# The order in which the residual's tiles are loaded for the down product of a SwiGLU sub-layer

## The chip, the cores and the metric

The kernel runs on one core of a Trainium2 chip. The metric is the device time of one execution in microseconds (us). Five engines work side by side: TensorE (PE in the profile, with its weight loads as PEld), VectorE (DVE), ScalarE (ACT), GpSimd (POOL) and SyncE (SP), which here issues almost every DMA. Each engine works its instructions off in the order in which they stand in the program.

## The reference, cut to what matters

The layer has a SwiGLU half-step at its start and another at its end. x has 1024 tokens of 1024 columns, the inner width is 2816, all in float32.

```python
def swiglu(h, w_gate, w_up, w_down):
    return (jax.nn.silu(h @ w_gate) * (h @ w_up)) @ w_down
...
        h = modulate(rms_norm(x, norm_ffn1[l]), mod[:, 0], mod[:, 1])
        x = x + 0.5 * mod[:, 2][:, None, :] * swiglu(h, ffn1_gate[l], ffn1_up[l], ffn1_down[l])
...
        h = modulate(rms_norm(x, norm_ffn2[l]), mod[:, 6], mod[:, 7])
        x = x + 0.5 * mod[:, 8][:, None, :] * swiglu(h, ffn2_gate[l], ffn2_up[l], ffn2_down[l])
```

The x that is added to is the residual. The product with w_down, and the sum with the residual, are the place of the change.

## The kernel before

Everything is held transposed: a tile has 128 columns of the layer (a row tile d, 0 to 7) and 512 tokens (a half h, 0 or 1). The residual is thus 16 tiles A[d, h] of 256 KB. While the gate and up products run, their place on the chip is needed for other things, so the residual waits in DRAM (`xpark` in the first half-step, `rest` in the second) and is loaded back for the down product.

The down product works on a pair p of row tiles (2p and 2p + 1) at a time and on both halves. It saves one block product in eight: `seven` makes seven products p1, p2, p5, p6, p3, p7 and q4 of sums and differences of blocks, each over a few pairs of inner tiles at once (an entry of the plan: the first four entries, for p = 0, 1, 2, 3, take 2, 3, 3 and 4 inner tiles). A float32 product is three matmuls of split values, so a product over 3 inner tiles is 9 matmuls. In the order of TensorE an entry's p1 stands ahead of the q4 of the entry before; then come the entry's p2, p5, p6, p3 and p7.

After a product, VectorE adds what stands in its PSUM bank, times fg (half the modulation vector), to a tile of the residual: `down_read`. p1 and p2 go to A[2p, 0], p5 to A[2p+1, 1], p6 and p3 to A[2p, 1], p7 to A[2p+1, 1] and q4 to A[2p+1, 0]. Products share banks: p6, p7 and q4 go on adding in the bank of p1 (`mm` in the profile), p3 in the bank of p5 (`po`). So p6 can't start before p1 has been read out, and p3 can't start before p5 has been read out; the read can't happen before its tile of the residual is there.

A tile of the residual takes one of 16 places called A0 to A15. Until shortly before, these hold values of the gate and up products, and some of them come free late: `direct_task` writes the last inner tiles straight from such a place (the VectorE instructions that write zs, G and H in the rows below) and gives it back. `feed_task` starts the loads, four tiles for each of the pairs 0 to 3, and feeds the ring of inner tiles (U, zs, G and H, loaded from `gd` in DRAM). `rest_load` waits for a free place, then issues its DMA.

The order of the work on each engine is made ahead of time: `Order` is a small planner that runs all tasks against estimated durations and writes down each engine's instructions in the order of its clock; tasks that wait for the same place get it in the order in which they were started. TensorE, VectorE and ScalarE keep that order. The order of the DMAs on SyncE's queue follows from when each can be issued.

Of the kernel before, what the change touches and what calls it, by code (L numbers as in the profile page):

```python
# [35 lines left out]
class Order:  # L36
# [18 lines left out]
    def spawn(self, gen, rank):  # L55
        self.seq += 1
        self.tasks.append({"gen": gen, "rank": rank, "seq": self.seq, "ready": self.t, "ask": None, "last": None, "end": self.t})
        return self.tasks[-1]
# [84 lines left out]
def hybrid_layer_kernel(  # L143
# [209 lines left out]
    spawn, put, mark = order.spawn, order.put, order.set  # L353

    def need(what, n=1):
        return ("need", what, n)

    def flag(*key):
        return ("flag", key)
# [22 lines left out]
    def temp(dt=F32):  # L382

        i = max(free, key=lambda i: (i % 8, i))
        free.remove(i)
        return i, atile(i, dt)
# [5 lines left out]
    def arrive(key, us=2.5):  # L392
        yield ("wait", us)
        mark(key)
# [357 lines left out]
    for st in range(2):  # L752
# [6 lines left out]
        for t in range(2 * NS):  # L759
            d = t % 4  # L760
# [358 lines left out]
    def place_of(v, r):  # L1119
        if v == "p5":  # L1120
            return utile(F32R), ztile(F32R)
        if v in ("p6", "p7"):
            return tuple(gtile((0 if v == "p6" else 8) + 2 * r + e, F32R) for e in range(2))
        ht = htile(r + (4 if v in ("p2", "p3") else 0), 1 if v in ("p3", "q4") else 0)
        return ht[:, 0], ht[:, 1]
# [17 lines left out]
    def feed_task(st):  # L1143

        for p in range(NPAIR):
            r = p % 4
            if p < 4:
                for d in (2 * p, 2 * p + 1):
                    for h in range(2):
                        spawn(rest_load(st, d, h), 2.5)  # L1150
            if p in DIRECT:
                continue
            for v in SLOTS if p < NS else ((0, 0), (0, 1), (1, 0), (1, 1)):
                place = v if p < NS else {(0, 0): "p1", (1, 0): "p2", (1, 1): "p3", (0, 1): "q4"}[v]
                if p < 4:
                    yield flag("vfree", st, place)
                else:
                    yield flag("gfree", st, p - 4, place)
                yield flag("gd", st, p, v)
                key = (st, p, v) if p < NS else (st, p, *v)  # L1160
                for e in range(2):
                    yield ("D", 0.78)
                    if e == 0:
                        ring[key] = place_of(place, r)
                    nc.sync.dma_start(out=ring[key][e].bitcast(F32), in_=gdram[st, p, v][:, e])
                spawn(arrive(("G", *key)), 3)

    def rest_load(st, d, h):

        yield flag("vfree", st, "p1")  # L1170
        while ("cut", st) not in order.flags and len(free) < 5:
            yield ("wait", 0.5)
        yield need("tmp")
        A[d, h] = temp()[1]
        yield ("D", 0.78)
        nc.sync.dma_start(out=A[d, h], in_=rest[st][d, h])
        spawn(arrive(("rest", st, (d, h))), 3)
# [861 lines left out]
    for st in range(2):  # L2039
        spawn(combine_task(st), 1.5)  # L2040
        for j in range(NPAIR):
            spawn(parts_task(st, j), 3.5)
        spawn(feed_task(st), 2.5)
# [41 lines left out]
```

## Time and profile before

| | |
|---|---|
| time, median of 3 runs | 1838.82 us (1838.65 to 1839.89) |
| time of the profiled execution | 1837.93 us |
| its span in the profile | 1836.2 us |
| mean granted TensorE clock | 0.996 of full |
| TensorE busy | 1791.9 us (98%) |
| VectorE busy | 1398.9 us (76%) |
| ScalarE busy | 759.8 us (41%) |
| GpSimd busy | 282.1 us (15%) |

Busy is the time in which an engine had an instruction in work. The profiled execution took 1.73 us more than its span, and 0.89 us less than the median. Times of single instructions are from the start of the span.

### The profile page before, as it was taken

Reading aid. Unit: us, or ns where it says so; the run is one execution under the profiler, and the core shown is the slowest. Engines: PE = TensorE matmul, PEld = TensorE weight load, DVE = VectorE, ACT = ScalarE, POOL = GpSimd, SP = SyncE. Lnnn points to the kernel's source line nnn. Section 1 sums busy time; section 2 is a strip of 40 time slices with the busy share of each in tenths; the row PEclk is TensorE's granted clock in tenths of the full one; section 3 lists DMA queues with packets and bytes.
Section 4 is the critical chain, followed back from the end, with each engine's and each line's share of the span. In section 5 each row is a group of like instructions: output and inputs, shape, how many; then the busy total and the mean of one; then the engine's idle time right before and its main releaser. Section 6 shows DMA issues by size and latency. Waiting matters only on the chain.

```text
span 1836.2 us, 25080 instructions
## 1 busy us (share of the span) xinstructions
PE 1791.9 (98%) x8527; PEld 1481.6 (81%) x8527; DVE 1398.9 (76%) x2434; ACT 759.8 (41%) x1504; POOL 282.1 (15%) x224
## 2 busy tenths in 40 slices
PE   7999999999999999999999999999999999999998
PEld 6788878888878876788888878888878888878877
DVE  5997888887769877988786666687787666776666
ACT  5454444443422224562443254354444444422223
POOL 2221121201100004120211122212211111100003
PEclk9999999999999999999999999999999999999999
DMA  9534676574679923321122155334455543758722
GB/s 326 176 127 161 217 223 196 184 231 134 204 227 337 320 87 118 104 74 48 27 52 50 35 164 156 100 125 155 150 189 169 185 152 110 228 179 274 235 76 98
DMA packets 307807, 293.81 MB, mean 160 GB/s; under 512 B 28061, under 2 KB 215506, under 8 KB 307680
## 3 DMA queue, kind: packets, MB, share of 16 engines
q1 hardware_dynamic: 307136, 291.09, 49.9%
q8 instruction: 67, 1.10, 0.3%
q0 software_dynamic: 544, 1.13, 0.2%
q14 instruction: 60, 0.49, 0.1%
HBM read 209.05 MB, written 83.10 MB: 159 GB/s over the span
## 4 chain that ended last, share of the span: by engine, by line
PE 85%; DVE 10%; issue 2%; ACT 1%; POOL 1%; DMA 1%; DVEq 0%; POOLq 0%; SPq 0%; ACTq 0%
PE mm L161 48%; PE po L161 27%; PE aux L161 7%; PE rec L161 3%; DVE pm L161 2%; DVE ad L161 2%; DVE A L161 1%; DVE split L161 1%; DVE G L161 1%; DVE cv L161 1%; DVE zs L161 0%; DVE H L161 0%; ACT A L161 0%; DMA G<-in_conv_w 0%; ACT junk L161 0%
## 5 line engine op out<-in xcount | busy, mean ns | idle before, releaser
L161 PE MATMUL mm<-H,split 128*128 128x512 f32 (+1 forms) x3096 | 759.2, 393 | 3.6 <-DVE A L161 3.6
L161 PEld LDWEIGHTS mm<-H,split 128*128 128x128 f32 x3096 | 566.4, 188 | 118.2 <-ACT split L161 4.6
L161 PE MATMUL po<-H,split 128*128 128x512 f32 x1584 | 390.2, 394 | 8.2 <-DVE A L161 6.1
L161 PEld LDWEIGHTS po<-H,split 128*128 128x128 f32 x1584 | 298.9, 190 | 73.4 <-ACT split L161 6.4
L161 PE MATMUL mm<-G,split 128*128 128x512 f32 x1440 | 342.3, 389 | 0.0
L161 PEld LDWEIGHTS mm<-G,split 128*128 128x128 f32 x1440 | 270.7, 188 | 56.3
L161 ACT CAST split<-pm 128x512 fp32r<-128x512 f32 (+3 forms) x264 | 151.7, 582 | 323.5 <-DVE pm L161 305.9
L161 POOL TENSOR_TENSOR A<-A,A 128x512 f32<-128x512 f32 x80 | 130.9, 1646 | 681.1 <-DVE A L161 456.9
L161 DVE TENSOR_TENSOR split<-pm,split 128x512 fp32r<-128x512 f32 (+3 forms) x264 | 176.7, 676 | 44.9 <-ACT split L161 44.5
L161 ACT CAST split<-raw 128x512 fp32r<-128x512 f32 (+3 forms) x199 | 117.6, 595 | 189.2 <-PE mm L161 106.4
L161 PE MATMUL po<-U,split 128*128 128x512 f32 x480 | 155.5, 390 | 2.1 <-DVE A L161 2.0
L161 DVE SCALAR_TENSOR_TENSOR A<-mm,fg,A 128x512 f32<-128x512 f32 (+1 forms) x144 | 103.4, 720 | 57.6 <-PE mm L161 55.8
L161 DVE TENSOR_TENSOR split<-raw,split 128x512 fp32r<-128x512 f32 (+3 forms) x199 | 131.6, 672 | 20.3 <-ACT split L161 19.9
L161 DVE TENSOR_TENSOR A<-A,A 128x512 fp32r<-128x512 f32 (+1 forms) x180 | 125.1, 703 | 4.0 <-ACT A L161 1.2
L161 PEld LDWEIGHTS po<-U,split 128*128 128x128 f32 x480 | 90.1, 188 | 22.0 <-issue 1.7
L161 ACT CAST split<-cv 128x512 fp32r<-128x512 f32 (+2 forms) x96 | 57.1, 595 | 91.5 <-PE po L161 55.8
L161 DVE TENSOR_TENSOR A<-A,po 128x512 f32<-128x512 f32 x86 | 58.8, 684 | 45.7 <-PE po L161 43.8
L161 PE MATMUL po<-zs,split 128*128 128x512 f32 x240 | 93.5, 390 | 0.0
L161 DVE SCALAR_TENSOR_TENSOR A<-po,fg,A 128x512 f32<-128x512 f32 x78 | 58.3, 749 | 37.6 <-PE po L161 37.3
L161 DVE SCALAR_TENSOR_TENSOR ad<-ad,cs,ad 128x512 f32<-128x512 f32 x98 | 82.8, 845 | 2.2 <-DMA ad<-in_w_ada 1.2
L161 DVE TENSOR_TENSOR split<-cv,split 128x512 fp32r<-128x512 f32 (+2 forms) x96 | 62.7, 653 | 28.3 <-ACT split L161 28.3
L161 ACT CAST A<-A 128x512 fp32r<-128x512 f32 x120 | 72.7, 619 | 25.3 <-DVE A L161 25.2
(270 smaller groups left out, 1856.4 us busy)
## 6 DMA issues: line engine op xcount, KB each, us to landing
gd<-A SPq DMA_DIRECT2D x240, 256.0 KB, 3.8
H<-gd SPq DMA_DIRECT2D x144, 256.0 KB, 4.3
ad<-in_w_ada SPq DMA_DIRECT2D x112, 256.0 KB, 3.1
raw<-in_ffn_gate SPq DMA_DIRECT2D x88, 256.0 KB, 3.9
cv<-in_ffn_up SPq DMA_DIRECT2D x80, 256.0 KB, 4.3
G<-gd SPq DMA_DIRECT2D x64, 256.0 KB, 4.7
raw<-in_w_in SPq DMA_DIRECT2D x40, 256.0 KB, 3.1
raw<-in_w_out SPq DMA_DIRECT2D x32, 256.0 KB, 3.1
```

What stands on the lines that cost most here:

```text
L161: ins = f(*args, **kwargs)
```

## The change

The four tiles of a pair are started in another order: before (2p, 0), (2p, 1), (2p+1, 0), (2p+1, 1), now (2p, 0), (2p+1, 1), (2p, 1), (2p+1, 0). This is the order in which the products p1, p5, p6 and q4 first read them. It holds for all four pairs and both half-steps.

```diff
             if p < 4:
-                for d in (2 * p, 2 * p + 1):
-                    for h in range(2):
-                        spawn(rest_load(st, d, h), 2.5)
+                for d, h in ((2 * p, 0), (2 * p + 1, 1), (2 * p, 1), (2 * p + 1, 0)):
+                    spawn(rest_load(st, d, h), 2.5)
```

The places come free at the same points as before, so what moves is which tile gets which place, and with it the planner's order. The order of TensorE's, ScalarE's and GpSimd's instructions is the same in both kernels; VectorE's differs in one stretch of some 20 instructions in each half-step. Both stretches are around the second entry with 3 inner tiles (p = 2, row tiles 4 and 5).

SyncE's queue in the first half-step, from the first load for row tiles 4 and 5 that stands late on. In DRAM, xpark_778 is A[4, 1], 723 is A[5, 0], 785 is A[5, 1]; 735, 792, 744 and 798 are A[6, 0], A[6, 1], A[7, 0] and A[7, 1]. A[4, 0] was loaded long before in both kernels. Before:

```order
L1176 DMA A_969_4726<-xpark_778 128x512
L1176 DMA A_972_4743<-xpark_723 128x512
...
L1176 DMA A_989_4830<-xpark_785 128x512
L1176 DMA A_990_4836<-xpark_735 128x512
L1176 DMA A_991_4841<-xpark_792 128x512
L1176 DMA A_994_4850<-xpark_744 128x512
L1176 DMA A_995_4861<-xpark_798 128x512
L1165 DMA H_0_1002_4904<-gd_1793 128x512 x2
```

The same place of the queue in the changed kernel:

```order
L1175 DMA A_969_4726<-xpark_785 128x512
L1175 DMA A_972_4743<-xpark_778 128x512
...
L1175 DMA A_989_4830<-xpark_723 128x512
L1175 DMA A_990_4844<-xpark_735 128x512
L1175 DMA A_993_4862<-xpark_798 128x512
L1164 DMA H_0_1000_4898<-gd_1793 128x512
L797 DMA cv_4892<-in_ffn_down 128x3x128
L1164 DMA H_0_1000_4898<-gd_1793 128x512
L1175 DMA A_1001_4904<-xpark_792 128x512
...
L1175 DMA A_1008_4937<-xpark_744 128x512
```

A[5, 1] has moved from the third to the first of these loads, A[4, 1] from the first to the second, A[5, 0] from the second to the third; the loads of A[6, 1] and A[7, 0] now stand among the loads of the ring and of weights.

VectorE's order at the same entry; po_4806 is the bank of p5 and p3, mm_4750 the bank of p1, p6 and p7, and the A in a row is the residual's tile that is added to. Before:

```order
L161 TENSOR_TENSOR zs_4629<-A_917_4525,U_4628 128x512
L161 TENSOR_TENSOR G_948_4638<-A_923_4544,G_947_4637 128x512
L161 TENSOR_TENSOR H_1_953_4654<-A_880_4331,H_1_953_4654 128x512
L161 TENSOR_TENSOR split_4825<-cv_4716,split_4825 128x512
L161 SCALAR_TENSOR_TENSOR A_969_4726<-mm_4750,fg_164,A_969_4726 128x512
L161 TENSOR_TENSOR pm_4844<-cv_4686,cv_4701 128x512
L161 TENSOR_TENSOR G_956_4667<-A_890_4377,G_955_4666 128x512
L161 SCALAR_TENSOR_TENSOR A_989_4830<-po_4806,fg_164,A_989_4830 128x512
```

In the changed kernel:

```order
L161 TENSOR_TENSOR zs_4629<-A_917_4525,U_4628 128x512
L161 SCALAR_TENSOR_TENSOR A_969_4726<-po_4806,fg_164,A_969_4726 128x512
L161 TENSOR_TENSOR split_4825<-cv_4716,split_4825 128x512
L161 TENSOR_TENSOR G_948_4638<-A_923_4544,G_947_4637 128x512
L161 SCALAR_TENSOR_TENSOR A_972_4743<-mm_4750,fg_164,A_972_4743 128x512
L161 TENSOR_TENSOR pm_4849<-cv_4686,cv_4701 128x512
L161 TENSOR_TENSOR H_1_953_4654<-A_880_4331,H_1_953_4654 128x512
L161 SCALAR_TENSOR_TENSOR A_972_4743<-po_4806,fg_164,A_972_4743 128x512
```

The read of p5 (the first with po_4806) has moved from behind the read of p6 (with mm_4750) to six instructions earlier, straight behind the instruction that writes zs; the read of p3 now stands where the read of p5 stood.

## Rows read from the trace of the kernel before

**Rows 1.** The page, part 1: busy us (share of the span) and instructions of TensorE.

```profile
PE 1791.9 (98%) x8527; PEld 1481.6 (81%) x8527; DVE 1398.9 (76%) x2434; ACT 759.8 (41%) x1504; POOL 282.1 (15%) x224
```

**Rows 2.** Waits of TensorE, whole span: us in total, times, longest us.

```profile
PE po L161 <- DVE A L161: 8.2, 6, 2.8
```

**Rows 3.** Timeline of TensorE, first half-step: start, us, what [idle before].

```profile
507.32 2.20 PE L161 MATMUL po<-H,split 128*128 128x512 f32 x9
...
511.40 2.20 PE L161 MATMUL mm<-G,split 128*128 128x512 f32 x9
516.40 3.67 PE L161 MATMUL po<-H,split 128*128 128x512 f32 x9 [2.80 <-DVE A L161]
519.87 2.49 PE L161 MATMUL mm<-G,split 128*128 128x512 f32 x9
522.20 4.93 PE L161 MATMUL mm<-H,split 128*128 128x512 f32 x21
...
545.33 2.20 PE L161 MATMUL po<-H,split 128*128 128x512 f32 x9
```

**Rows 4.** The chain that ended last, 455 to 560: start, us, what.

```profile
509.56 0.63 DVE A L161
...
510.23 0.55 DVE split L161
510.78 0.61 DVE zs L161
...
511.41 2.82 DMA A<-xpark
...
514.31 0.68 DVE pm L161
514.99 0.60 DVE G L161
515.59 0.67 DVE A L161
```

**Rows 5.** Timeline of VectorE, same place.

```profile
513.64 0.75 DVE L161 SCALAR_TENSOR_TENSOR A<-mm,fg,A 128x512 f32<-128x512 f32 x1 [0.46 <-PE mm L161]
...
520.11 0.75 DVE L161 SCALAR_TENSOR_TENSOR A<-po,fg,A 128x512 f32<-128x512 f32 x1 [2.66 <-PE po L161]
```

**Rows 6.** Timeline of SyncE's DMA issues, same place.

```profile
499.23 2.35 SPq L1176 DMA_DIRECT2D A<-xpark  x2
...
511.41 6.39 SPq L1176 DMA_DIRECT2D A<-xpark  x5
523.08 0.79 SPq L1165 DMA_DIRECT2D H<-gd  x2
```

**Rows 7.** Stretches: us, busy (x) of PE, PEld, DVE, ACT, POOL, clock, DMA share, GB/s.

```profile
516.40:519.87 3.47, 3.47 (x9) 2.72 (x10) 1.05 (x2) 0.00 (x0) 0.00 (x0) 0.58 0.55 151
527.00:545.00 18.00, 18.00 (x81) 14.92 (x80) 10.96 (x19) 3.71 (x7) 0.00 (x0) 1.00 0.97 326
1629.37:1633.04 3.67, 3.67 (x10) 2.85 (x10) 1.05 (x2) 0.00 (x0) 0.00 (x0) 0.55 0.47 144
```

**Rows 8.** Timeline of TensorE, second half-step.

```profile
1624.37 2.20 PE L161 MATMUL mm<-G,split 128*128 128x512 f32 x9
1629.37 3.87 PE L161 MATMUL po<-H,split 128*128 128x512 f32 x9 [2.80 <-DVE A L161]
1633.04 2.27 PE L161 MATMUL mm<-G,split 128*128 128x512 f32 x9
1635.15 4.92 PE L161 MATMUL mm<-H,split 128*128 128x512 f32 x21
```

**Rows 9.** The chain that ended last, 1585 to 1645.

```profile
1624.38 2.83 DMA A<-rest
```

**Rows 10.** The residual's tiles, 495 to 530: time from issue to landing.

```profile
DMA to landing us min/median/max: 2.5/2.8/3.5
```

**Rows 11.** The ring's loads from gd, 516 to 600: time from issue to landing.

```profile
DMA to landing us min/median/max: 2.5/5.2/7.2
```

## The prediction

> **What bounds the kernel now.** I read the page first: TensorE is busy for 1791.9 of 1836.2 us [rows 1], so the bound is TensorE's own work, and a change that adds or removes no matmul can only touch the few stretches in which TensorE stands still or runs slowly. Then the list of TensorE's waits: the longest entry is a product in a `po` bank that waits for VectorE to finish a tile A, 8.2 us in six waits, the longest 2.8 us [rows 2]. Reads in `down_read` are what writes A there, so I looked for these waits in the timeline of both down products. There are two of 2.80 us, at the same product of each half-step [rows 3, 8]: a product over 3 inner tiles with moving tiles H in a `po` bank, straight behind the product in `mm` with G. By the order of the program that is p3 of row tiles 4 and 5 behind p6. p3 goes on in the bank of p5, so it waits for the read of p5.
>
> The chain of waits says what that read waited for [rows 4]. VectorE's read at 509.56, a split and the instruction that writes zs follow each other; the last one frees a place at 511.39, a load of the residual is issued at 511.41 and lands 2.82 us later; then VectorE does pm, G and, at 515.5, the read of p5, and p3 starts at 516.40. The second half-step's chain has the same link, 2.83 us long [rows 9]. p5 itself was finished at 511.40, when p6 started [rows 3]. So a finished product lay in its bank for over 4 us because its tile of the residual was the third of a group of late loads, and because VectorE's order, which had allowed for that, put three other instructions ahead of the read.
>
> **The cost of that wait, now.** p2 starts at 507.32 and p6 at 511.40, so two products of 9 matmuls take 4.08 us, 2.04 each [rows 3]. p6 thus ends at 513.44 and p3 starts at 516.40: 2.96 us lost. Behind the gap TensorE is slow: p3 takes 3.47 us (516.40 to 519.87) at a granted clock of 0.58, mostly the lower level of 1.2 GHz, where the stretch after it has 1.00 [rows 7]. That is 1.43 us over 2.04; p7 (519.87 to 522.20) takes 2.33, 0.29 over. The first half-step loses 2.96 + 1.43 + 0.29 = 4.68 us. In the second [rows 8]: p6 ends at 1624.37 + 2.04 = 1626.41, p3 starts at 1629.37 (2.96), takes 3.67 at a clock of 0.55 [rows 7] (1.63 over), p7 2.11 (0.07 over): 4.66 us. Both together: 9.34 us.
>
> Is the clock's share, 1.72 and 1.70 us, there in every run? Both half-steps show it after equal gaps, and the three timed runs lie within 1.24 us of one another, less than one half-step's share. I count it in full; without it the gaps alone are 5.92 us.
>
> The Trainium skill, "TensorE: Matmul & The Clock Gate", Part 1, says that the moments at which the clock changes are not tied to the kernel's own course, so that the same gap need not cost the same clock in each run. By that page the saving would lie anywhere between the gaps alone and the full sum, and the runs would scatter; the trace and the runs show no such scatter.
>
> **The change, part by part.** No instruction is added or removed. The four loads of a pair are the same four DMAs; what they cost is only when they land.
>
> A[5, 1], which p5 needs: it takes the place whose load was issued at 499.23 [rows 6] instead of 511.41. Slowest landing of such a load: 3.5 us [rows 10], so it is there by 502.7, and p5 ends at 511.40. 8.7 us to spare.
>
> A[4, 1], which p6 needs: second of the two loads that end their issue at 499.23 + 2.35 = 501.58, there by 505.1; p6 ends at 513.44. 8.3 us to spare.
>
> A[5, 0], which q4 needs: it takes the late place, issued at 511.41, there by 514.9. q4 stands behind p3, p7 and the next entry's p1: with the gap gone it ends near 513.44 + 2.04 + 2.04 + 4.93 = 522.45 (4.93 is the row of p1 and q4 together [rows 3]). 7.5 us to spare.
>
> VectorE's order: the read of p5 now stands behind the instruction that writes zs, whose place in time I leave at 510.78 to 511.39 [rows 4]. It waits 0.2 us for p5's end and runs until about 512.4. p3 may start at 513.44: a spare of 1 us, the smallest in this sum. Behind the read stand a split and a G instruction, 0.6 each, so the read of p6, which began at 513.64 [rows 5], still finds VectorE free (512.4 + 1.2 = 513.6) and p7 has its bank by 514.4, when p3 is still running until 515.48. VectorE was idle for 2.66 us waiting for the late p3 [rows 5]; that idle time covers the instructions that are wanted earlier now.
>
> G has moved behind the read of p5, so the next place, for A[6, 0], comes free some 1.5 us later than before, about 513.5; its tile is there by 517 and p1 of that entry ends at about 513.44 + 4.08 + 2.82 = 520.3 (12 of the 21 matmuls that took 4.93 us [rows 3]). Covered by 3 us. A[7, 1], [6, 1] and [7, 0] follow in the order in which their products come, each behind a later VectorE instruction.
>
> Sum, against the profiled execution's own time: 1837.93 - 9.34 = 1828.59 us. That execution lay 0.89 us under the median, so for a median of the changed kernel I say 1829.5 us, 0.5% less. Bounds: nothing beyond the two stalls can be gained, since the other reads of these entries start as soon as their product ends; the low end of the range, 1828.0, leaves 1.5 us for the spread of runs. The least gain with the wait gone is the idle time without the clock, 5.92 us; it sets the range's high end.
>
> **The rivals.**
>
> 1. Only the idle time comes back, or the clock dips at some other point: 1838.82 - 5.92 = 1832.9. For it speaks only that the clock's price was read in one execution; against it the equal price in both half-steps, the clock of 1.00 in the stretch behind [rows 7] and the lack of another gap near the place. The Trainium skill's page on the clock gate, Part 1, as told above, would give this case more.
>
> 2. The transfers bind. From 527 to 545 the DMA engines are busy 0.97 of the time at 326 GB/s [rows 7]; if their pace sets when the ring's tiles arrive, TensorE would reach p2 of a later entry 4.68 us earlier and wait. Against it: no TensorE wait for a DMA shows there, and the ring's loads are released by TensorE itself, the first at 523.08 [rows 6], 0.88 us after p1 started on the tile that it replaces [rows 3], so they move forward with it. The first half-step would give its gain back: 1838.82 - 4.66 = 1834.2.
>
> 3. The wait changes its owner: something else holds p3 until 516. Candidates are the read of p5, whose spare is 1 us, and a weight split. Then nothing changes: 1838.8. Against it: the chain shows the load as what came last, and the splits of p3 and p7 stand ahead of the rows discussed, in both orders.
>
> 4. Slower: SyncE's queue is blocked. The loads of A[6, 1] and A[7, 0] now stand among those of the ring, and each waits for VectorE to free its place; what stands behind waits too. The last of them waits for an H instruction that stands three behind q4's read: 522.45 + 0.2 + 0.75 + 2 x 0.6 = 524.6 or so. Behind it stands half of the H tile that p2 needs at 545.33 - 4.68 = 540.65 [rows 3]; with 7.2 us for the slowest landing [rows 11] and 1 us of issues the spare is about 8 us. Past that each us costs one in each half-step; past 8 + 4.7 = 12.7 us of delay the kernel is slower than before. At 16 us it would take 1829.5 + 2 x 8 = 1845.5. I see nothing on VectorE that would hold it so long.
>
> **How the numbers follow.** Forecast, 1828 to 1831: 0.75. Rival 1: 0.08. Rival 2: 0.05. Rival 3: 0.06. Rival 4: 0.04. More gain than forecast: 0.02. A difference of 0.2% (3.7 us) is about what a measurement of this kernel can tell from no change. The forecast, rivals 1 and 2 and the larger gain are faster by more: 0.90. Rival 3 is the same: 0.06. Rival 4 is slower: 0.04. The range of 1828.0 to 1833.0 holds the forecast and rival 1, 0.83.
>
> **What would show it.** In the changed trace p3 of row tiles 4 and 5 should start 2.04 us after p6 in both half-steps, with no idle time for VectorE's A ahead of it, take 2.04 us, and the clock of that stretch should be 1.00. The DMA of a residual's tile should be gone from the chain at that place. The wait of `po` for A should fall from 8.2 to about 2.6 us. The prediction is wrong if p3 still waits there, if the clock still falls, or if a wait for a DMA shows up between 520 and 640.

## The result and the profile after

The changed kernel takes 1829.43 us (median of 5 runs, 1828.96 to 1831.54) where the kernel before took 1838.82 us (5 runs beside it): a ratio of 0.9949, 95% interval 0.9939 to 0.9960. The profiled execution took 1829.04 us with a span of 1827.3 us, 8.9 us less than the span before. The prediction said 1829.5 us, in a range of 1828.0 to 1833.0.

TensorE's timeline at the place of the first stall, in the changed kernel (start, us, what; answers to [rows 3]):

```profile
507.42 2.20 PE L161 MATMUL po<-H,split 128*128 128x512 f32 x9
511.50 2.20 PE L161 MATMUL mm<-G,split 128*128 128x512 f32 x9
513.54 2.20 PE L161 MATMUL po<-H,split 128*128 128x512 f32 x9
515.58 2.20 PE L161 MATMUL mm<-G,split 128*128 128x512 f32 x9
517.62 4.92 PE L161 MATMUL mm<-H,split 128*128 128x512 f32 x21
...
540.74 2.20 PE L161 MATMUL po<-H,split 128*128 128x512 f32 x9
```

p6, p3 and p7 now start 2.04 us after each other, with no idle time in brackets. The same place of the second half-step, answering to [rows 8]:

```profile
1620.04 2.20 PE L161 MATMUL mm<-G,split 128*128 128x512 f32 x9
1622.08 2.20 PE L161 MATMUL po<-H,split 128*128 128x512 f32 x9
1624.12 2.20 PE L161 MATMUL mm<-G,split 128*128 128x512 f32 x9
1626.16 4.92 PE L161 MATMUL mm<-H,split 128*128 128x512 f32 x21
```

p6 starts 4.33 us earlier than before, the gain of the first half-step less 0.36 us that were lost outside the two places; p1 of the next entry, three products later, starts 8.99 us earlier (1626.16 against 1635.15).

VectorE's timeline (answers to [rows 5]): the read of p5 stands directly behind the instruction that writes zs, and waits for TensorE alone.

```profile
510.79 0.68 DVE L161 TENSOR_TENSOR zs<-A,U 128x512 fp32r<-128x512 f32 x1
511.70 0.75 DVE L161 SCALAR_TENSOR_TENSOR A<-po,fg,A 128x512 f32<-128x512 f32 x1 [0.22 <-PE po L161]
...
513.80 0.75 DVE L161 SCALAR_TENSOR_TENSOR A<-mm,fg,A 128x512 f32<-128x512 f32 x1
...
515.78 0.75 DVE L161 SCALAR_TENSOR_TENSOR A<-po,fg,A 128x512 f32<-128x512 f32 x1
```

SyncE's issues (answers to [rows 6]): two loads of the residual at the old time, three where five stood, and the ring's first load 4.6 us earlier than the 523.08 of before.

```profile
499.33 2.35 SPq L1175 DMA_DIRECT2D A<-xpark  x2
...
511.50 4.59 SPq L1175 DMA_DIRECT2D A<-xpark  x3
518.49 0.32 SPq L1164 DMA_DIRECT2D H<-gd  x1
...
524.56 0.32 SPq L1175 DMA_DIRECT2D A<-xpark  x1
```

The chain of waits, 455 to 560 (answers to [rows 4]), holds TensorE alone; the DMA and VectorE's steps are gone from it:

```profile
507.58 4.08 PE po L161 x18
511.66 2.04 PE mm L161 x9
513.70 2.04 PE po L161 x9
515.74 6.80 PE mm L161 x30
```

TensorE's wait of `po` for A over the whole span (answers to [rows 2]; us, times, longest):

```profile
PE po L161 <- DVE A L161: 2.6, 4, 1.2
```

And the stretches (answers to [rows 7]; behind the length TensorE's busy time; third from the end the clock, then the busy share of the DMA engines and GB/s): the clock is 1.00 throughout, with the DMA engines as busy as before in the last:

```profile
513.40:522.30 8.90, 8.90 (x41) 7.38 (x40) 8.10 (x13) 2.38 (x4) 0.00 (x0) 1.00 0.50 153
527.00:545.00 18.00, 18.00 (x81) 14.92 (x80) 10.83 (x19) 3.59 (x7) 0.00 (x0) 1.00 0.97 325
```

### The profile page after: what moved, and what is told of

Its sections match the earlier page's. It is cut to its first block, busy times and chain, and to the rows that moved or that the text cites. A ratio compares the mean times of both kernels' runs of the same rounds, so it can differ in the third digit from the quotient of the medians.

```text
span 1827.3 us, 25078 instructions
## 1 busy us (share of the span) xinstructions
PE 1788.6 (98%) x8527; PEld 1479.5 (81%) x8527; DVE 1399.7 (77%) x2434; ACT 760.1 (42%) x1504; POOL 281.9 (15%) x224
## 4 chain that ended last, share of the span: by engine, by line
PE 85%; DVE 10%; issue 2%; ACT 1%; POOL 1%; DMA 0%; DVEq 0%; POOLq 0%; ACTq 0%
PE mm L161 48%; PE po L161 27%; PE aux L161 7%; PE rec L161 3%; DVE pm L161 2%; DVE ad L161 2%; DVE split L161 1%; DVE A L161 1%; DVE G L161 1%; DVE cv L161 1%; DVE H L161 1%; ACT A L161 0%; DVE zs L161 0%; DMA G<-in_gdn_norm 0%; ACT junk L161 0%
## 5 line engine op out<-in xcount | busy, mean ns | idle before, releaser
L161 PE MATMUL po<-H,split 128*128 128x512 f32 x1584 | 386.1, 391 | 2.2 <-DVE H L161 1.6
```

The lines of the kernel that those rows point to most:

```text
L161: ins = f(*args, **kwargs)
```

## Experiments

The theory: one stall in each half-step, at p3 of row tiles 4 and 5, is the whole gain, and it needs both an early tile and an early read. The rivals: the order of all four pairs counts; one of the two (tile, read) is enough; a half-step gives its gain back. The ratios below are each against runs of the kernel before on the same chip; those runs had medians of 1840.27 (pair 2 alone, the rest without pair 2, first half-step), 1840.15 (the last four) and 1838.46 us (second half-step).

| kernel | median us (runs) | ratio to before, 95% interval |
|---|---|---|
| pair 2 alone | 1831.57 (4) | 0.9952 (0.9936 to 0.9969) |
| all but pair 2 | 1839.50 (10) | 0.9997 (0.9988 to 1.0006) |
| first half-step alone | 1834.28 (8) | 0.9973 (0.9963 to 0.9983) |
| second half-step alone | 1834.11 (10) | 0.9975 (0.9966 to 0.9985) |
| early tile, late read | 1839.80 (10) | 1.0001 (0.9992 to 1.0011) |
| late tile, early read | 1833.59 (6) | 0.9967 (0.9955 to 0.9978) |
| p6's tile late | 1831.13 (4) | 0.9955 (0.9941 to 0.9970) |
| the changed kernel again | 1830.30 (4) | 0.9948 (0.9931 to 0.9965) |

**Which pair?** The new order for pair 2 alone, and its complement (`NEW` and `OLD` stand for the two orders of the change):

```diff
-                for d, h in NEW:
+                for d, h in NEW if p == 2 else OLD:
```

> The new load order for pair 2 alone (row tiles 4 and 5), in both half-steps; pairs 0, 1 and 3 keep the old one. Theory (one stall per half-step, p3 of pair 2 waiting for the read of p5): the whole gain of 9.3 us, 1829.5 us, no wait of a po product for A at that place. Rival (the order of all four pairs matters, each a part): about a quarter to a half of the gain, 1834 to 1837 us.

The complement is `OLD if p == 2 else NEW`.

> The complement: the new load order for pairs 0, 1 and 3, the old one for pair 2. Theory: both gaps of 2.80 us stay, no change, 1838.8 us within 0.1%. Rival (all pairs matter): half to three quarters of the gain, 1832 to 1834 us.

Pair 2 alone gives the whole gain (0.9952 against 0.9949 and 0.9948), the other three give nothing (0.9997). In the complement the gap stands where it stood:

```profile
511.04 2.20 PE L161 MATMUL mm<-G,split 128*128 128x512 f32 x9
516.04 3.61 PE L161 MATMUL po<-H,split 128*128 128x512 f32 x9 [2.80 <-DVE A L161]
519.44 2.54 PE L161 MATMUL mm<-G,split 128*128 128x512 f32 x9
521.82 4.92 PE L161 MATMUL mm<-H,split 128*128 128x512 f32 x21
```

So the order of the other pairs costs TensorE nothing here. It is not without effect: with pair 2 alone changed, VectorE's read of p5 of the next entry waits 1.79 us for its tile and starts 1.22 us after p5's end (531.04 against 529.82; in the changed kernel 0.20, 528.02 against 527.82). p3 of that entry still follows p6 without a gap, at 532.53.

**Do the half-steps add up?** The new order for `st == 0` alone, then for `st == 1` alone:

```diff
-                for d, h in NEW:
+                for d, h in NEW if st == 0 else OLD:
```

> The new load order in the first half-step alone. Theory: the two half-steps add up, so 4.7 us of the gain, 1834.1 us; the gap in the second half-step stays at 2.80 us with a clock near 0.55 behind it. Rival (the first half-step gives its gain back where the DMA engines are busy 0.97): no change, 1838.8 us.

> The new load order in the second half-step alone, the complement of the kernel with the first half-step changed. If the half-steps add up: 4.7 us less than the kernel before (a ratio of 0.9975); the gap of 2.80 us stays in the first half-step and is gone in the second. If the second half-step gives its part back, or if the first alone carried the gain: no change. If the gap's clock price depends on the run, p3 behind the first gap takes either about 3.4 us or 2.15 us.

Each gives about half (0.9973 and 0.9975: 5.0 and 4.6 us on the medians of before beside them; the differences of the medians themselves are 6.0 and 4.4). That the first half-step gives its gain back where the DMA engines are 0.97 busy is refuted. One thing was not as expected: with the first half-step changed, the gap in the second is as long as ever, but the clock did not fall behind it. p3 takes 2.15 us there (1626.76 to 1628.91):

```profile
1621.76 2.20 PE L161 MATMUL mm<-G,split 128*128 128x512 f32 x9
1626.76 2.32 PE L161 MATMUL po<-H,split 128*128 128x512 f32 x9 [2.80 <-DVE A L161]
1628.91 2.21 PE L161 MATMUL mm<-G,split 128*128 128x512 f32 x9
```

So this gap loses 3.08 us (2.96, and 0.12 of slower matmuls) instead of 4.66, and by the rows the kernel with the first half-step changed should gain 4.68 + 1.58 = 6.3 us, not 4.7. The interval of its ratio, 3.1 to 6.8 us, holds both.

With the second half-step changed, the gap in the first costs the clock as before (p3 517.01 to 519.70, p7 to 522.79: 5.78 us for the two where 4.08 would do):

```profile
517.01 2.89 PE L161 MATMUL po<-H,split 128*128 128x512 f32 x9 [2.80 <-DVE A L161]
519.70 3.26 PE L161 MATMUL mm<-G,split 128*128 128x512 f32 x9
522.79 4.94 PE L161 MATMUL mm<-H,split 128*128 128x512 f32 x21
```

**Tile or read?** The change does two things at once: it lands the tile early, and, through the planner, it moves VectorE's read ahead. They can be parted by what the planner is told of the landing. The changed kernel with A[5, 1] said to land late has early loads and the VectorE order of before:

```diff
-        spawn(arrive(("rest", st, (d, h))), 3)
+        spawn(arrive(("rest", st, (d, h)), 14.3 if (d, h) == (5, 1) else 2.5), 3)
```

> The changed kernel, but the planner is told that A[5, 1] lands 14.3 us after its issue instead of 2.5. The loads stay early; VectorE's read of p5 goes back behind the read of p6, pm and G, row for row as in the kernel before. If an early tile is enough, VectorE's order being a detail: 1829.5 us, no gap. If the read's place in VectorE's order is what counts once the tile is there: the gap stays near 2.8 us in both half-steps and the time is 1838.8 us. I expect the second.

No gain at all: 1.0001. The load is issued at 501.21, so the tile is there some 9 us before p5 ends, and TensorE waits as before, because VectorE reaches the read too late. SyncE's, TensorE's and VectorE's rows:

```profile
501.21 2.36 SPq L1175 DMA_DIRECT2D A<-xpark  x2
...
513.39 2.20 PE L161 MATMUL mm<-G,split 128*128 128x512 f32 x9
518.44 3.53 PE L161 MATMUL po<-H,split 128*128 128x512 f32 x9 [2.85 <-DVE A L161]
...
515.68 0.75 DVE L161 SCALAR_TENSOR_TENSOR A<-mm,fg,A 128x512 f32<-128x512 f32 x1 [0.51 <-issue]
516.35 0.68 DVE L161 TENSOR_TENSOR pm<-cv,cv 128x512 f32<-128x512 f32 x1
516.95 0.68 DVE L161 TENSOR_TENSOR G<-A,G 128x512 fp32r<-128x512 f32 x1
517.55 0.74 DVE L161 SCALAR_TENSOR_TENSOR A<-po,fg,A 128x512 f32<-128x512 f32 x1
```

VectorE's read of p6 comes first (515.68) and can't start before p6 has ended, at 513.39 + 2.04 = 515.43. Behind it stand pm, G and the read of p5, so p3 has to wait although its tile has long been there.

The other way round, the kernel before with A[5, 1] said to land at once (the load itself stays where it was):

```diff
-        spawn(arrive(("rest", st, (d, h))), 3)
+        spawn(arrive(("rest", st, (d, h)), 0.0 if (d, h) == (5, 1) else 2.5), 3)
```

> The kernel before, but the planner is told that A[5, 1] lands at once. The load stays late (issued at about 511.4, there at 514.2); VectorE's read of p5 moves ahead of the read of p6, a split, pm and G, and VectorE stands still until the tile is there. By the chain the read then runs from 514.25 to 514.9 and p3 starts at about 515.05: a gap of 1.6 us instead of 2.96 in each half-step. If the clock falls behind this gap as behind the longer one (1.7 us): 1838.8 - 2 x 1.36 = 1836.1 us. If it does not fall: 1838.8 - 2 x 3.06 = 1832.7 us. Rival (VectorE's order alone is the gain): 1829.5 us.

The ratio is 0.9967, that is 6.1 us, as expected for a shorter gap without a fall of the clock (1838.8 to 1832.7). The rows say 5.6: the two places lose 1.91 and 1.80 us where they lost 4.68 and 4.66. Its chain of waits at that place:

```profile
513.86 0.61 DVE zs L161
...
514.49 2.79 DMA A<-xpark
...
517.40 0.76 DVE A L161
...
518.30 2.32 PE po L161 x9
```

VectorE's read now follows the landing (514.49 + 2.79) within 0.12 us, and p3 follows the read. The stretches behind the gaps (1.62 us in the first half-step, 1.51 in the second) show p3 at 2.16 us and the clock at 1.00:

```profile
518.30:520.46 2.16, 2.16 (x9) 1.77 (x10) 2.16 (x4) 0.34 (x1) 0.00 (x0) 1.00 0.00 1
1628.77:1630.93 2.16, 2.16 (x10) 1.76 (x10) 2.16 (x4) 0.34 (x1) 0.00 (x0) 1.00 0.02 6
```

So the read's place in VectorE's order was the larger part of the loss, together with the clock; an early tile is worth something only once the read may use it, and takes away the rest.

**Is it enough that p5's tile is early?** The last two of the four loads exchanged, so that the tile of p6 and p3 gets the late place:

```diff
-                for d, h in ((2 * p, 0), (2 * p + 1, 1), (2 * p, 1), (2 * p + 1, 0)):
+                for d, h in ((2 * p, 0), (2 * p + 1, 1), (2 * p + 1, 0), (2 * p, 1)):
```

> The changed kernel with the last two tiles of each pair exchanged: (2p, 0), (2p+1, 1), (2p+1, 0), (2p, 1), so that the tile of p6 and p3 gets the late place (issued at 511.4, there at 514.2) and that of q4 the early one. p3 no longer waits; but VectorE's read of p6 moves behind pm, H and G, to 515.3 to 516.0, and p7 wants the bank at 515.5. Expected: a gap of about 0.65 us ahead of p7 in each half-step, too short to lower the clock: 1.3 us over the changed kernel, 1830.7 us. Rival (only the tile of p5 matters): 1829.4 us, no gap.

> The changed kernel once more, on the same chip as the runs beside it, as their yardstick: 1829.4 us.

The stall moves on by one product, to p7, which waits for the read of p6:

```profile
512.98 2.20 PE L161 MATMUL po<-H,split 128*128 128x512 f32 x9
515.74 2.32 PE L161 MATMUL mm<-G,split 128*128 128x512 f32 x9 [0.56 <-DVE A L161]
517.90 4.93 PE L161 MATMUL mm<-H,split 128*128 128x512 f32 x21
```

p7 starts 2.76 us after p3 and takes 2.16, at a clock of 1.00: 0.84 us lost (0.65 was expected), and the second half-step's row is alike (a gap of 0.57). The medians of the two kernels on that chip differ by 0.8 us (1831.13 and 1830.30) where the rows say 1.7; the intervals overlap, so the times don't tell the two apart. The trace shows the loss at this place, and by it the order p5, p6, q4 of the change is the better one of the two.

**How often does the gap cost the clock?** Three more traced executions of the kernel before, and one more of the kernel with the first half-step changed.

> The kernel before, unchanged, looked at again, to see how often its two gaps of 2.80 us cost the clock. If they always do (the prediction counted 1.72 and 1.70 us in full): p3 takes about 3.5 us at a clock of 0.55 to 0.62 in both half-steps, in all three looks. If it depends on the run, as in the second half-step of the kernel with the first half-step changed (clock 1.00): some of the six gaps show p3 at about 2.15 us, and such an execution is about 1.6 us shorter for each.

> As in the first look: always about 3.5 us for p3 behind both gaps, or 2.15 us behind some.

> As in the first look: always about 3.5 us for p3 behind both gaps, or 2.15 us behind some.

> The kernel with the first half-step changed, looked at again: its gap of 2.80 us in the second half-step either costs the clock this time (p3 about 3.5 us) or again does not (2.15 us).

The three executions took 1840.71, 1838.09 and 1840.17 us. All six gaps cost the clock; the second execution's two are

```profile
516.63 3.20 PE L161 MATMUL po<-H,split 128*128 128x512 f32 x9 [2.80 <-DVE A L161]
519.63 2.97 PE L161 MATMUL mm<-G,split 128*128 128x512 f32 x9
522.43 4.93 PE L161 MATMUL mm<-H,split 128*128 128x512 f32 x21
...
1629.51 3.31 PE L161 MATMUL po<-H,split 128*128 128x512 f32 x9 [2.80 <-DVE A L161]
1632.62 2.85 PE L161 MATMUL mm<-G,split 128*128 128x512 f32 x9
1635.31 4.93 PE L161 MATMUL mm<-H,split 128*128 128x512 f32 x21
```

Both times p3 and p7 take 5.80 us together, 1.72 over; how the loss is shared between the two products differs from one execution to the next, its sum hardly (1.46 us was the least of the six). In the other kernel's second execution (1832.27 us) the gap of 2.80 us again cost nothing: p3 ran from 1625.31 to 1627.47.

## Why the prediction was right

**What bounds the kernel.** TensorE's two gaps behind p6 were the whole of it. They are gone, pair 2 alone takes them away, and the other pairs change nothing that can be measured.

**What held the read.** Here the prediction read too much into the chain. It named the load's landing as what came last, and the late tile as the first reason for the wait. In the kernel before, the tile landed at 511.41 + 2.82 = 514.23, and VectorE started pm, directly behind its read of p6, at 514.31 [rows 4, 5]: two paths ended within 0.1 us of each other, and the chain followed one of them. Its argument against rival 3 rests on the same reading. With the tile early and VectorE's order kept, the landing is out of the way and the gap is 2.85 us instead of 2.80. So VectorE's order alone accounts for the whole wait, and the lateness of the tile set it only through the planner, which had put the read behind the time at which it expected the tile. The lateness costs time by itself only when the read stands early: 1.91 and 1.80 us. The number came out right because the change removes both; an early load under the old order of VectorE would have promised the same 9.34 us by this chain, and gives nothing.

**The cost of the wait.** The sum was 4.68 + 4.66 = 9.34 us. The medians differ by 9.39 us, the two profiled spans by 8.9. At p2 of the later entry the changed kernel is 4.59 us ahead (540.74 against 545.33), of which 0.10 was lost at the start (507.42 against 507.32), so the first half-step gave 4.69 us; the second gave 8.99 - 4.33 = 4.66 us. Both terms are right to a hundredth of a us or so. The spans differ by 0.45 us less than the two together: 0.10 us were lost ahead of the first place, 0.26 between the two, and the rest behind.

**The clock's share** was counted in full, 3.42 us of the sum, because both half-steps showed it after equal gaps. For the kernel before this holds in all four traced executions (8 gaps of 8); in another kernel of this case two gaps of 2.80 us had no fall behind them. "TensorE: Matmul & The Clock Gate", Part 1, in the Trainium skill says that the chip's watch on activity runs free of the kernel, so that one kernel can have different numbers of slow matmuls from run to run; the two gaps without a fall agree with it. The choice was right for the median, but the argument for it from the spread of three runs was weak: the runs of the kernel before beside the experiments spread from 1836.9 to 1841.0 us on one chip and from 1835.5 to 1841.3 on another. Nor does the spread tell the price of these gaps: the first and the second of the three further traced executions differ by 2.62 us, while their gaps cost 9.11 and 9.36 us; p6 of the first half-step starts 1.39 us later in the first, and another 1.43 us are lost between the two places. In two of the 45 runs beside the experiments (1836.90 and 1835.46 us) the mean clock was 0.998, in the others 0.992 to 0.996; whether the gaps kept the clock there, no trace tells.

**The tiles and VectorE's order.** The times came out as worked out: the read of p5 from 511.70 (said: p5's end and 0.2), that of p6 at 513.80 (said: 513.6), the last load of the residual at 524.56 (said: about 524.6). That the read's place matters was a clause of the working; the experiments show it to be the half without which the other is worth nothing.

**The rivals.** Idle time alone (1832.9): refuted, the clock's share came back as well. (The early read with the late tile took 1833.59 us, close to it by chance: there the clock did not fall, and part of the idle time stayed.) Transfers bind: refuted, each half-step keeps its part. The wait changes its owner: no other wait stands there; with p6's tile late it does move, to p7. SyncE's queue blocked: the last load among the ring's went out within 0.1 us of the time worked out, and no wait of VectorE or TensorE for one of these loads shows. As a sign of being wrong the prediction named a wait for a DMA between 520 and 640. Taken by the letter, there are some: ScalarE's splits wait for DMAs five times there, 7.5 us in all, where it was once and 1.5 us before. TensorE waits for no DMA there, and the gain stays.

## What to carry to other kernels

When a finished PSUM bank holds up the next product, look for what its reader waits for, and follow both ends: when the operand lands, and where the read stands in its engine's order; moving one without the other gave nothing here (the tile), or about two thirds (the read). Where a chain names a landing, see whether the engine that waits for it would have come any earlier without it: here two paths ended within 0.1 us of each other. Of loads that start as places come free, the one that is read first should get the first place, and only where places come free late does it count: one pair of four. And price a gap of TensorE by the rows behind it too: 2.96 us of idle time were in most cases followed by 1.7 us of slow matmuls.

## What the runs showed of the hardware that was not expected

Gaps of TensorE that the profile gives as 2.80 or 2.85 us were followed by a fall of the granted clock in 13 of 15 cases (two each in four executions of the kernel before, in the kernel with all but pair 2 changed and in the one with an early tile and a late read, one in the kernel with the second half-step changed), each time with 1.46 to 1.73 us lost; in the two others, both in the second half-step of the kernel whose first half-step had no gap, the clock stayed at 1.00. What sets these two apart was not found: the gap and the products around it are alike, and in the first of them the DMA engines are 0.47 busy behind the gap, as in the kernel before. Two executions can't tell the kernel from the single run. Gaps of 1.62, 1.51, 0.57 and 0.56 us, each seen in one trace, were not followed by a fall. Where the clock stayed at 1.00, behind the long gaps and the short ones, the first product of 9 matmuls took 2.15 or 2.16 us instead of 2.04.
